# A two-layer decoder trunk: full-height query/key splits laid out by DMA, and attention outputs kept in device memory

## The chip, the cores and the metric

The kernel runs on one core of one Trainium2 chip. The metric is the device time of one execution in microseconds (us). In what follows PE is the matrix engine (TensorE), DVE the vector engine, ACT the scalar engine, POOL the GpSimd engine, and SP the engine whose queue issues the DMAs. Each engine works through its own queue of instructions in order; an instruction whose inputs are not ready holds up all that stand behind it on that engine.

## The reference

The reference is a trunk of two layers on 512 positions of width 1024. Each layer is a token mixer, a squared-ReLU MLP and a gated input embedding. Cut to the part that the change touches:

```python
for i in range(2):
    hn = rmsnorm(h, norm_mix_g[i])
    if i == 0: h = h + even_mixer(hn, ...)   # 8 stick-breaking heads, 4 differential heads (2 maps each)
    else:      h = h + odd_mixer(hn, ...)    # 16 dilated heads, T5 bias added to the logits
    ...                                      # MLP, gated embedding
# in a mixer
q, k, v = split(hn @ w_in)                   # heads of 64 columns
sc = q @ k.T * scale (+ bias[rel])           # causal
o = softmax(sc) @ v                          # or stick-breaking weights, or a difference of two softmaxes
return o @ w_out
```

All of it is in fp32.

## The kernel before

A product in fp32 is made as three products of parts (`mm3`, L135): every operand is split into `hi`, its value rounded to the PE's fp32r type, and `lo`, what is left over; then hi·hi, hi·lo and lo·hi are added in PSUM. Activations lie transposed, features on the 128 partitions and the 512 positions along the free axis.

A mixer works on four groups of four heads (two pairs for the differential kind). For a group, `project` (L398) runs the V, Q and K projections, each from a 1 MB block of weights that is loaded by one DMA (`wload`, L112, two buffers `raw`) and split by ACT into `wh` (L122) and by POOL into `wl` (L126), with three buffers of each. The first group of a layer takes Q and K before V. Q and K each have two halves of 128 rows (two heads of 64 rows). `attend` (L538) makes the steps of the attention of a group: scores, softmax or scan, a transpose, the product with V. The projection of one group is interleaved with the attention of the group before (`interleave`, L157); a scheduler settles each engine's queue from that. So PE always has projection matmuls to set between the attention's short ones, and the scores of a group can start when the K half of that group has been laid out.

The layout is made by `evacuate` (L457). `f` is the projected half, scaled, in fp32 (DVE, L460, tile `tmp`, one buffer). The score of a head is two matmuls over 128 partitions: the stationary `qq` holds the head's q hi in one half of the partitions and q lo in the other, the moving operand is once `kh` (k hi in both halves) and once `klz` (k lo in the half of q hi, zeros in the other, L493 and L494). A Q half takes 2 ACT copies and 2 DVE subtractions on 64 partitions (L466, L467); a K half takes 4 ACT copies and 2 DVE subtractions (L474 to L476).

All DMAs are issued on SP's queue, in the order in which the scheduler set them: weight blocks (L114), bias tiles (L500, three buffers), projections of the embedding put to device memory (L356, tile `pjd`) and fetched later. `prepare` (L308), after the first group's projection in layer 0, makes the rows from which the bias tiles are read: it loads a table, one-hot rows and offsets (L311 to L316) and lambdas (L319), runs four small matmuls (L323), writes the rows to device memory (`urow`, L326). The softmax of a score (DVE, L508) needs its bias tile.

Attention outputs stay in eight tiles of SBUF (`oT`, L396). Six of them are split and go through the output projection (`out_first`, L630, and `spread`, L624) under the last group's attention; the last two follow at the end of the mixer.

Of the kernel before, what the change touches and what calls it, by code (L numbers as in the profile page):

```python
# [12 lines left out]
F32 = mybir.dt.float32  # L13
F32R = mybir.dt.float32r
I32 = mybir.dt.int32
AF = mybir.ActivationFunctionType
ALU = mybir.AluOpType
AX = mybir.AxisListType

P = 128  # L20
D = 1024
S = 512
KT = D // P
# [39 lines left out]
def trunk(  # L63
# [5 lines left out]
    nc = tc.nc  # L69
    uid = [0]  # L70

    def nm(s):
        uid[0] += 1
        return f"{s}_{uid[0]}"

    cpool = ctx.enter_context(tc.tile_pool(name="cpool", bufs=1))
    dpool = ctx.enter_context(tc.tile_pool(name="dpool", bufs=1, space=bass.MemoryType.DRAM))
    wpool = ctx.enter_context(tc.tile_pool(name="wpool", bufs=2))
    apool = ctx.enter_context(tc.tile_pool(name="apool", bufs=8))
    spool = ctx.enter_context(tc.tile_pool(name="spool", bufs=8))  # L80
# [2 lines left out]
    def const(shape, name, dtype=F32):  # L83
        return cpool.tile(shape, dtype, tag=name, name=name)

    T_BUFS = {"e": 5, "tmp": 1, "tmp2": 3}

    mix = []

    def t2k(tag, pool=None, dtype=F32):  # L90
        return (pool or (mix[0] if tag in ("tmp", "tmp2") else spool)).tile([P, S], dtype, tag=tag, name=nm(tag), bufs=T_BUFS.get(tag, 2))

    def col(name="c"):
        return spool.tile([P, 1], F32, tag="col", name=nm(name), bufs=24)
# [3 lines left out]
    def ps(tag):  # L98
        return psum.tile([P, S], F32, tag=tag, name=nm(tag), bufs=PS_BUFS[tag])
# [12 lines left out]
    def wload(src):  # L112
        raw = wpool.tile([P, src.shape[-1]], F32, tag="raw", name=nm("raw"), bufs=2)
        nc.sync.dma_start(raw, src)  # L114
        return raw
# [19 lines left out]
    def mm3(acc, lh, ll, rh, rl, start, stop):  # L135
        nc.tensor.matmul(acc, lh, rh, start=start, stop=False)  # L136
        nc.tensor.matmul(acc, lh, rl, start=False, stop=False)  # L137
        nc.tensor.matmul(acc, ll, rh, start=False, stop=stop)  # L138
# [30 lines left out]
    def split_tile(src, scale=None, bufs=8):  # L169
        hi = apool.tile([P, S], F32R, tag="hi", name=nm("hi"), bufs=bufs)  # L170
        lo = apool.tile([P, S], F32R, tag="lo", name=nm("lo"), bufs=bufs)
        if scale is None:
            nc.scalar.activation(hi, src, AF.Copy)
            nc.vector.tensor_tensor(lo, src, hi.bitcast(F32), op=ALU.subtract)
        else:
            last_split[:] = [nc.scalar.activation(hi, src, AF.Copy, scale=scale).ins]
            nc.vector.scalar_tensor_tensor(lo, src, scale, hi.bitcast(F32), op0=ALU.mult, op1=ALU.subtract)  # L177
        return hi, lo
# [159 lines left out]
    def ple_units(layer):  # L338
        raw = wpool.tile([P, 2 * KT * P], F32, tag="raw", name=nm("raw"), bufs=2)
        nc.sync.dma_start(raw[:, 0:2 * S].rearrange("p (k c) -> p k c", k=2), pT[layer].rearrange("k p c -> p k c"))  # L340
        ph, pl = wsplit(raw, 0, 2, S)
        raw = wload(w_proj[layer])
        for c in range(2):
            wh, wl = wsplit(raw, c, 2, 512)
            for i in range(4):
                acc = ps("mm")
                sl = slice(i * P, (i + 1) * P)
                for k in range(2):
                    if layer < DEPTH - 1:
                        mm3(acc, wh[:, k, sl], wl[:, k, sl], ph[:, k], pl[:, k], k == 0, k == 1)  # L350
                    else:
                        mm3(acc, ph[:, k, sl], pl[:, k, sl], wh[:, k], wl[:, k], k == 0, k == 1)
                    yield 2.0
                t = t2k("tmp2")
                nc.scalar.activation(t, acc, AF.Copy)
                nc.sync.dma_start(pjd[layer, 4 * c + i], t)  # L356

    KLB = 2
    kl_i = [0]


    def mixer(layer, norm, nxt):
        st = ExitStack()
        mpool = st.enter_context(tc.tile_pool(name=f"mpool{layer}", bufs=2))
        mix[:] = [mpool]

        klz = [[mpool.tile([P, S], F32R, tag=f"klz{s}{x}", name=nm("klz"), bufs=1) for x in range(KLB)]
               for s in range(2)]
        for x in range(KLB):
            nc.gpsimd.memset(klz[0][x][64:128].bitcast(F32), 0.0)  # L370
            nc.gpsimd.memset(klz[1][x][0:64].bitcast(F32), 0.0)
        NSLOT = 13
        pth = [mpool.tile([P, NSLOT, P], F32R, tag=f"pth{i}", name=nm("pth"), bufs=1) for i in range(2)]
        ptl = [mpool.tile([P, NSLOT, P], F32R, tag=f"ptl{i}", name=nm("ptl"), bufs=1) for i in range(2)]
# [18 lines left out]
            return w_in[layer, nblk[0] - 1]  # L393

        first = []
        oT = [mpool.tile([P, S], F32, tag=f"o{k}", name=nm("o"), bufs=1) for k in range(KT)]  # L396

        def project(g, cur):  # L398
            kind = "dil" if layer else ("sb" if g < 2 else "diff")
# [33 lines left out]
            heads = []  # L433
# [23 lines left out]
            def evacuate(isq, i, acc, qk, qscale):  # L457
                rstd = stat["rstd"]
                f = t2k("tmp")
                nc.vector.scalar_tensor_tensor(f, acc, qscale if isq else -0.5, rstd, op0=ALU.mult, op1=ALU.mult)  # L460
                lower, upper = slice(0, 64), slice(64, 128)
                if isq:
                    qq = []
                    for a, b in ((lower, upper), (upper, lower)):
                        q = mpool.tile([P, S], F32R, tag="qq", name=nm("qq"), bufs=6)
                        nc.scalar.activation(q[a], f[a], AF.Copy)  # L466
                        nc.vector.tensor_tensor(q[b], f[a], q[a].bitcast(F32), op=ALU.subtract)  # L467
                        qq.append(q)
                    qk.append(qq)
                else:  # L470
                    for s, (a, b) in enumerate(((lower, upper), (upper, lower))):
                        kl = klz[s][kl_i[0] % KLB]
                        kh = mpool.tile([P, S], F32R, tag="kh", name=nm("kh"), bufs=5)
                        nc.scalar.activation(kh[a], f[a], AF.Copy)  # L474
                        nc.scalar.activation(kh[b], f[a], AF.Copy)
                        nc.vector.tensor_tensor(kl[a], f[a], kh[a].bitcast(F32), op=ALU.subtract)  # L476
                        heads.append((qk[i][s], kh, kl))
                    kl_i[0] += 1
            cur.extend((g, kind, v, heads))
            if start:  # L480
                wide_i[0] = 0
# [56 lines left out]
        def attend(g, kind, v, heads):  # L538
# [37 lines left out]
            def combine(x):  # L576
                hi, lo = pth[pts[x]], ptl[pts[x]]
                if kind == "diff":
                    vh = lambda j: v[:, j, P * x:P * x + P]
                    vl = lambda j: v[:, j, 256 + P * x:256 + P * x + P]  # L580
                    op = pv([(vh, hi), (vh, lo), (vl, hi)])
                    o = oT[2 * g + x]
                    nc.scalar.activation(o, op, AF.Copy)
                    return
                vs = lambda j: v[:, j, P * x:P * x + P]
                op = pv([(vs, hi), (vs, lo)])
                a = slice(64 * (x % 2), 64 * (x % 2) + 64)
                b = slice(64 - 64 * (x % 2), 128 - 64 * (x % 2))
                o = oT[2 * g + x // 2]
                nc.scalar.activation(o[a], op[b], AF.Copy)  # L590
                nc.vector.tensor_tensor(o[a], op[a], o[a], op=ALU.add)

            def subnorm(x):
                o = oT[2 * g + x]
                hi, rs, lo = t2k("tmp2", dtype=F32R), t2k("tmp2"), t2k("tmp2", dtype=F32R)
                nc.scalar.activation(rs, o, AF.Square)
                nc.scalar.activation(hi, rs, AF.Copy)
                nc.vector.tensor_tensor(lo, rs, hi.bitcast(F32), op=ALU.subtract)
                mp = ps("pv")
                nc.tensor.matmul(mp, ones_r, hi, start=True, stop=False)  # L600
                nc.tensor.matmul(mp, ones_r, lo, start=False, stop=True)
                rsqrt(rs, t2k("tmp2"), mp, SUBLN_EPS, eps_s, scale=float(D // P))
                nc.vector.scalar_tensor_tensor(o, o, gsub, rs, op0=ALU.mult, op1=ALU.mult)

            def step(n):
                m = n - LAG
# [10 lines left out]

            return [(lambda n=n: step(n)) for n in range(QT * nh + LAG + PVLAG + (kind == "diff"))]

        groups = GROUPS[layer]  # L620
        tiles = [2 * g + d for g in groups for d in range(2)]
        ohl = []

        def spread(units, every):  # L624
            for x, cost in enumerate(units):
                if x % every == 0 and len(ohl) < 6:
                    ohl.append(split_tile(oT[tiles[len(ohl)]]))
                yield cost

        def out_first():  # L630
            ohl.extend(split_tile(oT[k]) for k in tiles[len(ohl):6])
            for c in range(4):
                for i, ws in enumerate(block(w_outa[layer, c], 6, P)):
                    acc = ps("mm")
                    yield from lin_units([acc], [ws], ohl, 0, 6, False)
                    nc.vector.tensor_tensor(h[2 * c + i], h[2 * c + i], acc, op=ALU.add)
# [364 lines left out]
```

## Time and profile before

| | |
|---|---|
| median of 3 runs (lowest, highest) | 1314.71 us (1312.79, 1315.17) |
| profiled execution, its own time | 1313.5 us |
| its span in the trace | 1311.6 us |
| PE busy | 1280.7 us (98% of the span) |
| DVE busy | 982.5 us (75%) |
| ACT busy | 686.4 us (52%) |
| POOL busy | 189.0 us (14%) |
| mean granted PE clock | 0.999 |
| DMAs on SP's queue | 198 rows, 132 MB |

The span is the time between the first and the last instruction in the trace. A busy time adds up the stretches in which an engine works at an instruction; what an engine is short of the span it waited or had nothing to do.

### The profile page before, as it was taken

The numbers are of one execution on the slowest core, as the hardware profiler recorded it, in microseconds if no ns is written. First come the engines' busy times: TensorE is split into PE (matmuls) and PEld (weight loads), VectorE is DVE, ScalarE is ACT, GpSimd is POOL, SyncE is SP. The second block draws the span as 40 slices with busy tenths as digits, with TensorE's granted clock in tenths as the row PEclk, the third lists the DMA queues.
The fourth block names the chain that finished last, engine by engine and source line by source line (L and its number), as shares of the span: only waits on it lengthen the run. The fifth ranks groups of instructions, "written<-read, shape, count | busy, mean of one in ns | idle before, by whom it ended". The sixth has DMA issues, their size and how long they took to land.

```text
span 1311.6 us, 18552 instructions
## 1 busy us (share of the span) xinstructions
PE 1280.7 (98%) x7224; PEld 1112.5 (85%) x7224; DVE 982.5 (75%) x1669; ACT 686.4 (52%) x1117; POOL 189.0 (14%) x160
## 2 busy tenths in 40 slices
PE   8999999999999999999999999999999999999997
PEld 6878787788998989988889899878899898898886
DVE  6688888867858859945667878886795795994566
ACT  6566768654534435334456667765454443433344
POOL 2333343420000000000014333332000000000001
PEclk9999999999999999999999999999999999999999
DMA  5321323223232232322432232211323223232241
GB/s 208 123 91 55 114 95 107 89 82 111 97 116 78 97 129 71 122 97 96 161 121 103 64 114 76 72 65 64 129 78 116 96 97 113 81 129 96 97 145 65
DMA packets 28041, 133.21 MB, mean 102 GB/s; under 512 B 3312, under 2 KB 4048, under 8 KB 15280
## 3 DMA queue, kind: packets, MB, share of 16 engines
q1 hardware_dynamic: 27952, 132.01, 29.0%
q8 instruction: 57, 0.93, 0.3%
q14 instruction: 32, 0.26, 0.1%
HBM read 125.63 MB, written 6.37 MB: 101 GB/s over the span
## 4 chain that ended last, share of the span: by engine, by line
PE 78%; DVE 12%; ACT 7%; issue 2%; DMA 1%; SPq 0%; ACTq 0%; DVEq 0%
PE mm L137 12%; PE mm L138 12%; PE mm L136 12%; PE tp L138 5%; PE tp L136 5%; PE tp L137 5%; PE sc L136 4%; PE sc L137 4%; PE sc L138 4%; PE pv L137 2%; PE pv L136 2%; PE pv L138 2%; PE pv L534 2%; DVE e L572 2%; PE tp L519 1%
## 5 line engine op out<-in xcount | busy, mean ns | idle before, releaser
L122 ACT ACTIVATE wh<-raw 128x1024 fp32r<-128x1024 f32 (+1 forms) x168 | 173.5, 1037 | 230.1 <-PE mm L137 72.6
L136 PE MATMUL mm<-hi,wh 128*128 128x512 f32 x564 | 222.3, 394 | 0.9 <-ACT wh L302 0.9
L126 POOL TENSOR_TENSOR wl<-raw,wh 128x512 fp32r<-128x512 f32 (+1 forms) x132 | 176.3, 1358 | 318.4 <-ACT wh L122 301.7
L137 PE MATMUL mm<-lo,wh 128*128 128x512 f32 x564 | 220.6, 391 | 0.3 <-DVE lo L177 0.3
L138 PE MATMUL mm<-hi,wl 128*128 128x512 f32 x564 | 220.5, 391 | 0.3 <-DVE wl L128 0.3
L128 DVE TENSOR_TENSOR wl<-raw,wh 128x1024 fp32r<-128x1024 f32 x102 | 124.4, 1222 | 40.3 <-ACT wh L122 33.9
L138 PEld LDWEIGHTS mm<-hi,wl 128*128 128x128 f32 x564 | 105.9, 188 | 23.5 <-DVE wl L128 0.7
L137 PEld LDWEIGHTS mm<-lo,wh 128*128 128x128 f32 x564 | 106.0, 188 | 20.9 <-DVE lo L177 1.5
L136 PEld LDWEIGHTS mm<-hi,wh 128*128 128x128 f32 x564 | 105.9, 188 | 20.5 <-ACT wh L302 1.1
L725 ACT ACTIVATE wh<-raw 128x1024 fp32r<-128x1024 f32 x48 | 50.7, 1057 | 70.7 <-PE sc L137 35.5
L138 PE MATMUL mm<-uh,wl 128*128 128x256 f32 (+1 forms) x288 | 86.6, 301 | 0.0
L137 PE MATMUL mm<-ul,wh 128*128 128x256 f32 (+1 forms) x288 | 86.6, 301 | 0.0
L136 PE MATMUL mm<-uh,wh 128*128 128x256 f32 (+1 forms) x288 | 86.6, 301 | 0.0
L511 ACT ACTIVATE e<-e,mn 128x128 f32<-128x128 f32 (+3 forms) x96 | 53.8, 560 | 52.2 <-DVE mn L508 51.9
L704 DVE TENSOR_TENSOR ul<-u,uh 128x1792 fp32r<-128x1792 f32 (+1 forms) x32 | 58.4, 1824 | 23.4 <-ACT uh L703 23.4
L703 ACT ACTIVATE uh<-u 128x1792 fp32r<-128x1792 f32 (+1 forms) x32 | 49.4, 1543 | 48.4 <-DVE u L699 48.2
L692 ACT ACTIVATE u<-u 128x512 f32<-128x512 f32 x64 | 39.4, 624 | 53.4 <-DVE u L691 53.4
L726 DVE TENSOR_TENSOR wl<-raw,wh 128x1024 fp32r<-128x1024 f32 x48 | 58.6, 1221 | 9.8 <-ACT wh L725 9.7
L138 PE MATMUL sc<-hi,wl 128*128 128x512 f32 x168 | 65.6, 390 | 0.0
L137 PE MATMUL sc<-lo,wh 128*128 128x512 f32 x168 | 65.4, 389 | 0.0
L136 PE MATMUL sc<-hi,wh 128*128 128x512 f32 x168 | 65.4, 389 | 0.0
L137 PE MATMUL mm<-wl,hi 128*128 128x256 f32 (+1 forms) x216 | 64.1, 297 | 0.4 <-DVE wl L128 0.4
(255 smaller groups left out, 3463.9 us busy)
## 6 DMA issues: line engine op xcount, KB each, us to landing
raw<-in_w_up_dram SPq DMA_DIRECT2D x32, 1024.0 KB, 4.8
raw<-in_w_down_dram SPq DMA_DIRECT2D x32, 1024.0 KB, 4.9
raw<-in_w_in_dram SPq DMA_DIRECT2D x23, 1024.0 KB, 4.9
raw<-in_w_gate_dram SPq DMA_DIRECT2D x8, 1024.0 KB, 5.0
bias<-urow SPq DMA_DIRECT2D x24, 256.0 KB, 3.3
raw<-in_w_outa_dram SPq DMA_DIRECT2D x8, 768.0 KB, 4.2
pjd<-tmp SPq DMA_DIRECT2D x16, 256.0 KB, 2.2
pj<-pjd SPq DMA_DIRECT2D x16, 256.0 KB, 4.0
```

The lines of the kernel that those rows point to most:

```text
L122: nc.scalar.activation(hi, src, AF.Copy)
L126: nc.gpsimd.tensor_tensor(lo[:, kx], src[:, kx], hi[:, kx].bitcast(F32), op=ALU.subtract)
L128: nc.vector.tensor_tensor(lo, src, hi.bitcast(F32), op=ALU.subtract)
L136: nc.tensor.matmul(acc, lh, rh, start=start, stop=False)
L137: nc.tensor.matmul(acc, lh, rl, start=False, stop=False)
L138: nc.tensor.matmul(acc, ll, rh, start=False, stop=stop)
L511: nc.scalar.activation(e[:, 0:n], e[:, 0:n], AF.Exp, scale=-1.0, bias=mn, accum_out=s)
L692: nc.scalar.activation(ui, ui, AF.Square, scale=0.5)
L703: nc.scalar.activation(uh[:, parts], u[:, parts], AF.Copy)
L704: nc.vector.tensor_tensor(ul[:, parts], u[:, parts], uh[:, parts].bitcast(F32), op=ALU.subtract)
L725: nc.scalar.activation(hi, src, AF.Copy)
L726: nc.vector.tensor_tensor(lo, src, hi.bitcast(F32), op=ALU.subtract)
```

## The change

`evacuate` splits a half by one full-height ACT copy and one full-height DVE subtraction into two tiles `hl` (four buffers), and lays the parts out by DMAs from SBUF to SBUF, 64 partitions by 512 columns (128 KB) each: 4 for a Q half, 8 for a K half, 24 for a group. `kl` now holds k lo in both halves, as `kh` holds k hi, so the tiles with zeros and their memsets are gone. The output tiles rotate through five buffers; each of the first six of a layer is put to device memory when it is done (`put_out`) and fetched back before it is split (`fetch`): 12 puts and 12 fetches of 256 KB in all. In `ple_units` every second tile comes from the `hl` buffers.

```diff
-    T_BUFS = {"e": 5, "tmp": 1, "tmp2": 3}
+    T_BUFS = {"e": 5, "tmp": 1, "tmp2": 3, "hl": 4, "o": 5}
...
-                t = t2k("tmp2")
+                t = t2k("hl" if i % 2 else "tmp2")
                 nc.scalar.activation(t, acc, AF.Copy)
                 nc.sync.dma_start(pjd[layer, 4 * c + i], t)
...
-        klz = [[mpool.tile([P, S], F32R, tag=f"klz{s}{x}", name=nm("klz"), bufs=1) for x in range(KLB)]
-               for s in range(2)]
-        for x in range(KLB):
-            nc.gpsimd.memset(klz[0][x][64:128].bitcast(F32), 0.0)
-            nc.gpsimd.memset(klz[1][x][0:64].bitcast(F32), 0.0)
...
                 f = t2k("tmp")
                 nc.vector.scalar_tensor_tensor(f, acc, qscale if isq else -0.5, rstd, op0=ALU.mult, op1=ALU.mult)
+                hi, lo = t2k("hl", dtype=F32R), t2k("hl", dtype=F32R)
+                nc.scalar.activation(hi, f, AF.Copy)
+                nc.vector.tensor_tensor(lo, f, hi.bitcast(F32), op=ALU.subtract)
                 lower, upper = slice(0, 64), slice(64, 128)
                 if isq:
                     qq = []
-                    for a, b in ((lower, upper), (upper, lower)):
+                    for s in (lower, upper):
                         q = mpool.tile([P, S], F32R, tag="qq", name=nm("qq"), bufs=6)
-                        nc.scalar.activation(q[a], f[a], AF.Copy)
-                        nc.vector.tensor_tensor(q[b], f[a], q[a].bitcast(F32), op=ALU.subtract)
+                        nc.sync.dma_start(q[lower].bitcast(F32), hi[s].bitcast(F32))
+                        nc.sync.dma_start(q[upper].bitcast(F32), lo[s].bitcast(F32))
                         qq.append(q)
                     qk.append(qq)
                 else:
-                    for s, (a, b) in enumerate(((lower, upper), (upper, lower))):
-                        kl = klz[s][kl_i[0] % KLB]
-                        kh = mpool.tile([P, S], F32R, tag="kh", name=nm("kh"), bufs=5)
-                        nc.scalar.activation(kh[a], f[a], AF.Copy)
-                        nc.scalar.activation(kh[b], f[a], AF.Copy)
-                        nc.vector.tensor_tensor(kl[a], f[a], kh[a].bitcast(F32), op=ALU.subtract)
-                        heads.append((qk[i][s], kh, kl))
-                    kl_i[0] += 1
+                    for x, s in enumerate((lower, upper)):
+                        both = []
+                        for tag, part in (("kh", hi), ("kl", lo)):
+                            k = mpool.tile([P, S], F32R, tag=tag, name=nm(tag), bufs=4)
+                            nc.sync.dma_start(k[lower].bitcast(F32), part[s].bitcast(F32))
+                            nc.sync.dma_start(k[upper].bitcast(F32), part[s].bitcast(F32))
+                            both.append(k)
+                        heads.append((qk[i][x], *both))
...
+        def put_out(k):
+            if k in tiles[:6]:
+                nc.sync.dma_start(od[k], oT[k])
+
+        def fetch():
+            if len(back) < 6:
+                back.append(t2k("o"))
+                nc.sync.dma_start(back[-1], od[tiles[len(back) - 1]])
+
+        def split_out():
+            if not back:
+                for _ in range(2):
+                    fetch()
+            ohl.append(split_tile(back[len(ohl)]))
+            fetch()
```

Rows on SP's queue go from 198 to 414. Three places of the scheduled queues follow; in them `raw` is a weight block, and numbers tell tiles of one name apart.

The first is SP's queue in layer 1, where the first group's attention gives way to the second's. Before, the load of the third group's K weights (`raw_7716`) stands between bias loads:

```order
L500 DMA bias_7406<-urow 128x512
L500 DMA bias_7544<-urow 128x512
L114 DMA raw_7716<-in_w_in_dram 128x2048
L500 DMA bias_7658<-urow 128x512
L114 DMA raw_7872<-in_w_in_dram 128x2048
```

With the change the eight copies of the second group's first K half stand directly behind the same load (`raw_7869` here):

```order
L496 DMA bias_7687<-urow 128x512
L114 DMA raw_7869<-in_w_in_dram 128x2048
L471 DMA kh_7340<-hl_7336 64x512
L472 DMA kh_7340<-hl_7336 64x512
L471 DMA kl_7343<-hl_7337 64x512
L472 DMA kl_7343<-hl_7337 64x512
L471 DMA kh_7346<-hl_7336 64x512
L472 DMA kh_7346<-hl_7336 64x512
L471 DMA kl_7349<-hl_7337 64x512
L472 DMA kl_7349<-hl_7337 64x512
L628 DMA od<-o_7328 128x512
```

So what ACT and DVE wrote in place is now issued by SP after that load. The same eight rows stand behind the next group's load of the same kind, 33 rows later; at the third such place of layer 1 a bias load and four fetches stand ahead of them, and no weight block.

The second is PE's queue at the same place: the product with V of the old group's last head, the third group's V projection (`mm`), and the first score (`sc`) of the new group. Before:

```order
L534 MATMUL pv_7255<-ptl_6471,v_6476 128x256
L136 MATMUL mm_7279<-wh_7281,hi_6087 128x256
L137 MATMUL mm_7279<-wl_7282,hi_6087 128x256
L138 MATMUL mm_7279<-wh_7281,lo_6088 128x256
L493 MATMUL sc_7291<-kh_7210,qq_7022 128x256
L494 MATMUL sc_7291<-klz_6361,qq_7022 128x256
L136 MATMUL mm_7279<-wh_7281,hi_6098 128x256
```

With the change:

```order
L530 MATMUL pv_7389<-ptl_6471,v_6476 128x256
L136 MATMUL mm_7422<-wh_7424,hi_6194 128x256
L137 MATMUL mm_7422<-wl_7425,hi_6194 128x256
L138 MATMUL mm_7422<-wh_7424,lo_6195 128x256
L136 MATMUL mm_7422<-wh_7424,hi_6205 128x256
L137 MATMUL mm_7422<-wl_7425,hi_6205 128x256
L138 MATMUL mm_7422<-wh_7424,lo_6206 128x256
L136 MATMUL mm_7422<-wh_7424,hi_6277 128x256
L137 MATMUL mm_7422<-wl_7425,hi_6277 128x256
L489 MATMUL sc_7434<-kh_7340,qq_7142 128x256
L138 MATMUL mm_7422<-wh_7424,lo_6278 128x256
```

The first score moved back by five matmuls; its second product, with `kl`, stands 13 rows behind it. The next group's transition has the same order.

The third is SP's queue at the start of layer 0, where `prepare` loads its rows (`e`) and lambdas (`tmp`). Before:

```order
L311 DMA e_514<-in_t_table_dram 32x16
L312 DMA e_511<-in_onehot_dram 32x512
L313 DMA e_514<-in_onehot_dram 32x128
L315 DMA e_512<-in_offs_dram 16x512
L315 DMA e_513<-in_offs_dram 16x512
L316 DMA e_514<-in_offs_dram 16x2x128
L114 DMA raw_968<-in_w_in_dram 128x2048
L319 DMA tmp_515<-in_lambdas_dram 128x256
```

With the change, all 24 copies of the first group stand between the second and the third of these loads:

```order
L311 DMA e_523<-in_t_table_dram 32x16
L312 DMA e_520<-in_onehot_dram 32x512
L462 DMA qq_324<-hl_320 64x512
L463 DMA qq_324<-hl_321 64x512
...
L471 DMA kl_393<-hl_387 64x512
L472 DMA kl_393<-hl_387 64x512
L313 DMA e_523<-in_onehot_dram 32x128
L315 DMA e_521<-in_offs_dram 16x512
L315 DMA e_522<-in_offs_dram 16x512
```

On PE, the 96 matmuls of the second group's V projection and 42 of its Q projection move ahead of the third score, which before stood behind some 60 matmuls of V alone; by the end of the second group's K projection the two orders have the same work behind them.

## Rows read from the trace of the kernel before

**Rows 1.** Page, part 1: busy time, share of the span, instructions.

```profile
PE 1280.7 (98%) x7224; PEld 1112.5 (85%) x7224; DVE 982.5 (75%) x1669; ACT 686.4 (52%) x1117; POOL 189.0 (14%) x160
```

**Rows 2.** Busy time by stretch: PE, PEld, DVE, ACT, POOL, clock, DMA share, GB/s.

```profile
50.00:100.00 50.00, 47.50 (x274) 40.14 (x273) 37.77 (x99) 32.65 (x71) 15.99 (x13) 1.00 0.31 101
200.00:250.00 50.00, 47.37 (x235) 37.79 (x233) 44.16 (x75) 35.97 (x76) 19.01 (x15) 1.00 0.31 106
750.00:800.00 50.00, 50.00 (x304) 44.19 (x303) 40.48 (x103) 35.11 (x78) 18.44 (x14) 1.00 0.25 85
```

**Rows 3.** Waits of PE, 0 to 310 us: total, times, longest.

```profile
PE tp L519 <- DVE ptl L524: 4.1, 6, 1.3
PE sc L493 <- DVE mn L508: 3.5, 3, 1.8
PE sc L493 <- ACT e L569: 2.4, 3, 1.2
...
PE sc L323 <- DVE v L431: 1.7, 1, 1.7
```

**Rows 4.** Waits of PE, 660 to 960 us.

```profile
PE sc L493 <- DVE mn L508: 1.3, 1, 1.3
PE sc L493 <- DVE v L431: 0.7, 1, 0.7
```

**Rows 5.** Groups by shape, `evacuate`: busy, mean ns | idle before, releaser.

```profile
L476 DVE TENSOR_TENSOR klz<-tmp,kh 64x512 fp32r<-64x512 f32 x32 | 33.6, 1049 | 7.9 <-ACT kh L474 7.5
L467 DVE TENSOR_TENSOR qq<-tmp,qq 64x512 fp32r<-64x512 f32 x32 | 31.9, 998 | 3.8 <-ACT qq L466 3.0
...
L475 ACT ACTIVATE kh<-tmp 64x512 fp32r<-64x512 f32 x32 | 20.1, 629 | 0.7
```

**Rows 6.** Timeline near 154 us, ACT then PE: start, duration, idle before.

```profile
151.71 0.63 ACT L475 ACTIVATE kh<-tmp 64x512 fp32r<-64x512 f32 x1
...
154.14 0.45 PE L493 MATMUL sc<-kh,qq 128*128 128x384 f32 x1 [1.18 <-ACT e L569]
```

**Rows 7.** Timeline 748 to 756 us: ACT, DVE, POOL, SP, PE.

```profile
748.01 1.05 ACT L122 ACTIVATE wh<-raw 128x1024 fp32r<-128x1024 f32 x1
...
748.78 0.67 DVE L460 SCALAR_TENSOR_TENSOR tmp<-mm,rstd 128x512 f32<-128x512 f32 x1
...
749.13 3.00 POOL L126 TENSOR_TENSOR wl<-raw,wh 128x512 fp32r<-128x512 f32 x2 [6.82 <-ACT wh L122]
...
752.16 0.33 SPq L114 DMA_DIRECT2D raw<-in_w_in_dram  x1
...
754.98 0.28 PE L493 MATMUL sc<-kh,qq 128*128 128x256 f32 x1
755.10 0.28 PE L494 MATMUL sc<-klz,qq 128*128 128x256 f32 x1
```

**Rows 8.** DMA issues, median us to landing: 752 to 752.5 us; then 166 to 170 us.

```profile
raw<-in_w_in_dram SPq DMA_DIRECT2D x1, 1024.0 KB, 5.0
...
raw<-in_w_in_dram SPq DMA_DIRECT2D x1, 1024.0 KB, 5.4
pjd<-tmp SPq DMA_DIRECT2D x1, 256.0 KB, 5.6
```

**Rows 9.** SP's timeline, 167.5 to 169 us; the page's DMA issues.

```profile
167.93 0.34 SPq L114 DMA_DIRECT2D raw<-in_w_in_dram  x1
168.38 0.37 SPq L356 DMA_DIRECT2D pjd<-tmp  x1
...
pjd<-tmp SPq DMA_DIRECT2D x16, 256.0 KB, 2.2
```

**Rows 10.** Timeline 40 to 54 us: PE, then DVE.

```profile
46.96 0.39 PE L323 MATMUL sc<-e 32*16 32x128 f32 x2 [1.68 <-DVE v L431]
...
40.87 0.69 DVE L460 SCALAR_TENSOR_TENSOR tmp<-sc,rstd 128x512 f32<-128x512 f32 x1
...
53.92 0.29 DVE L508 CUSTOM_DVE_ANT_0 e<-sc,bias 128x128 f32<-128x128 f32 x1 [2.50 <-PE mm L138]
```

More of the change, by code (lines that the diff above doesn't have):

```diff
@@ L84, in const @@
         return cpool.tile(shape, dtype, tag=name, name=name)
-    T_BUFS = {"e": 5, "tmp": 1, "tmp2": 3}
+    T_BUFS = {"e": 5, "tmp": 1, "tmp2": 3, "hl": 4, "o": 5}
     mix = []
     def t2k(tag, pool=None, dtype=F32):
-        return (pool or (mix[0] if tag in ("tmp", "tmp2") else spool)).tile([P, S], dtype, tag=tag, name=nm(tag), bufs=T_BUFS.get(tag, 2))
+        return (pool or (mix[0] if tag in ("tmp", "tmp2", "hl", "o") else spool)).tile([P, S], dtype, tag=tag, name=nm(tag), bufs=T_BUFS.get(tag, 2))
     def col(name="c"):
@@ L353, in ple_units @@
                     yield 2.0
-                t = t2k("tmp2")
+                t = t2k("hl" if i % 2 else "tmp2")
                 nc.scalar.activation(t, acc, AF.Copy)
                 nc.sync.dma_start(pjd[layer, 4 * c + i], t)
-    KLB = 2
-    kl_i = [0]
+    od = dpool.tile([KT, P, S], F32, tag="od", name="od")
     def mixer(layer, norm, nxt):
@@ L395, in mixer @@
         first = []
-        oT = [mpool.tile([P, S], F32, tag=f"o{k}", name=nm("o"), bufs=1) for k in range(KT)]
+        oT = {}
         def project(g, cur):
@@ L581, in combine @@
                     op = pv([(vh, hi), (vh, lo), (vl, hi)])
-                    o = oT[2 * g + x]
+                    o = oT[2 * g + x] = t2k("o")
                     nc.scalar.activation(o, op, AF.Copy)
@@ L588, in combine @@
                 b = slice(64 - 64 * (x % 2), 128 - 64 * (x % 2))
+                if x % 2 == 0:
+                    oT[2 * g + x // 2] = t2k("o")
                 o = oT[2 * g + x // 2]
@@ L591, in combine @@
                 nc.vector.tensor_tensor(o[a], op[a], o[a], op=ALU.add)
+                if x % 2:
+                    put_out(2 * g + x // 2)
             def subnorm(x):
@@ L603, in subnorm @@
                 nc.vector.scalar_tensor_tensor(o, o, gsub, rs, op0=ALU.mult, op1=ALU.mult)
+                put_out(2 * g + x)
             def step(n):
@@ L621, in mixer @@
         tiles = [2 * g + d for g in groups for d in range(2)]
-        ohl = []
+        ohl, back = [], []
+        def put_out(k):
[11 more added lines that the diff above has]
+            fetch()
         def spread(units, every):
@@ L626, in spread @@
                 if x % every == 0 and len(ohl) < 6:
-                    ohl.append(split_tile(oT[tiles[len(ohl)]]))
+                    split_out()
                 yield cost
         def out_first():
-            ohl.extend(split_tile(oT[k]) for k in tiles[len(ohl):6])
+            while len(ohl) < 6:
+                split_out()
             for c in range(4):
```

## The prediction

> **What bounds the kernel now.** I read the page's busy times first. PE is busy 1280.7 of 1311.6 us [rows 1], so at most 31 us of the span are idle on PE, and only time added to PE's queue or taken out of its waits counts. Then busy time by stretch, to see which parts of the mixers have slack: in layer 0 PE misses 2.5 us between 50 and 100 and 2.6 between 200 and 250, where DVE is busy 44.2 of 50 us; in layer 1, from 750 to 800, PE misses nothing at all, though DVE does 40.5 of 50 [rows 2]. So in layer 1 there is nothing to win, and any new wait is a plain loss; in layer 0 there is a little to win from a lighter DVE and ACT. Then the waits of PE, for what that little is made of: in layer 0 tp behind DVE's ptl 4.1 us, scores behind DVE's softmax 3.5, scores behind ACT's e 2.4, one wait of 1.7 of a small matmul behind a v [rows 3]; in layer 1 1.3 and 0.7 [rows 4]. Last the timelines of ACT, DVE, POOL, SP and PE where one group's attention gives way to the next, since the edit sits there.
>
> The sum is made against the profiled execution, 1313.5 us; the median of the runs shown, 1314.7, is 1.2 above it, and I add the difference found to the median.
>
> **What is taken away.** The half-height operations go: 64 on DVE with 33.6 and 31.9 us busy, and 96 on ACT of 0.63 us, of which one of three groups is shown [rows 5]. Full-height ones over the same 512 columns replace them, 32 on each engine. I take one to cost as much as a half-height one, since the columns are as many. DVE then loses 65.5/2 = 32.7 us over eight groups, 4.1 a group; ACT 64 x 0.63 = 40 us, 5.0 a group. None of this is PE time, so it is worth what it takes out of PE's waits:
> - The score at 154.14 waited 1.18 us for ACT's e, and ACT had come from the last of its four kh copies at 152.34 [rows 6]. With one copy in place of four it is about 1.9 us earlier there. Of the 2.4 us of such waits [rows 3] I take 1.8 off.
> - The small matmul of `prepare` that waited 1.7 us for a v [rows 3, 10] now stands 75 rows behind its fellow, with projection work between: 1.7 off.
> - The wait of layer 1's first score for a v, 0.7 [rows 4], lies behind the same subtractions on DVE: 0.7 off.
> - The waits for DVE's ptl and softmax, 4.1 + 3.5 + 1.3 = 8.9 us [rows 3, 4]. DVE sheds 4.1 of about 41 us a group, a tenth, but the waits are chains that pass through ACT too. I take 2.0 off; the bounds are 0 and 8.9.
>
> Together 6.2 us, with bounds 0 and 13.7. The eight memsets on POOL were on no path.
>
> **What is added, layer 1.** SP now issues the copies, in order. At the transition before 755 us two chains start from the last matmul of a K half: the projection's f (DVE, 748.78 to 749.45), and the release of a `wh` buffer, so ACT's L122 at 748.01, POOL's L126 until 752.13, and then SP's load of a K block at 752.16 [rows 7]. With the change the second half of the first chain, the eight copies, stands on SP directly behind that load. The split itself could be done near 751 (0.67 for f, then 0.63 and 0.69), so the copies wait for the load to be issued, and then for its bytes. The load lands 5.0 us after its issue, at 757.16 [rows 8]. What a 256 KB transfer does right behind a 1 MB load is shown at 168 us: the load issued at 167.93 landed after 5.4, at 173.33; pjd, issued at 168.38, took 5.6 and landed at 173.98, 0.65 behind it, where pjd's median is 2.2 [rows 8, 9]. So the small transfer waited in line for the large one. The two copies of kh are 256 KB too: they land at about 757.16 + 0.65 = 757.8. PE came to its first score at 754.98 [rows 7]; five more matmuls stand ahead of it now, at 0.12 us each by the starts of such matmuls [rows 7]: 755.6. The stall is 2.2 us. The kl copies land 0.65 later, at 758.5; their matmul stands 13 rows on, at 757.8 + 1.6 = 759.4, and doesn't wait. Bounds: if copies did not stand in line, they would land 2.2 after an issue at 753.1 (two issues at the pace of 0.45 of rows 9), 755.3, and nothing is lost; if each needed pjd's 5.6 from there, 758.7, and 3.1 is lost. The same order stands at the next group's transition, 48 us later; at the third no weight block is ahead. Two stalls: 4.4 us, with bounds 0 and 6.2. PE had no idle time there to take it up [rows 2].
>
> What would a half-height copy cost? [...] No row here shows a copy on 64 partitions between tiles of SBUF. [...]
>
> **What is added, layer 0.** At the start, 24 copies stand between two loads of `prepare`. The last eight follow the second K half, whose f starts at 40.87 [rows 10]; split, it is ready near 43, and eight issues at 0.45 end at 46.6, four more loads at 48.4, and they land 2.2 to 5.6 later [rows 8, 9]: 50.6 to 54. Before, it was 7.0 us from the small matmul at 46.96 to the first softmax at 53.92 [rows 10]; so the first softmax comes at 57.6 to 61, 4 to 7 us late. PE has the second group's V and most of a Q half to do meanwhile, so it doesn't stall then. But the attention of the first group is pressed into less time: DVE's 37.8 us [rows 2], less 4.1, in 39 to 42 us, 80 to 87%, about the load at which PE misses 2.6 us in 50 from 200 to 250, against 2.5 already missed here [rows 2]. I take 1.5; the bounds are 0 (hidden) and 7 (nothing is made up).
>
> Other transitions of layer 0 have their copies landed 1 us or more before the first score by the same reckoning. The 12 puts and 12 fetches of 256 KB lie on SP under projections that are tens of us long; the fetches are asked for before the output projection's weights. A copy of the embedding's projection on ACT can wait for an `hl` buffer that the copies still read. 0.5 us for all that, with bounds 0 and 2.
>
> **Sum.** 4.4 + 1.5 + 0.5 - 6.2 = +0.2 us: 1313.7 against 1313.5, or 1314.9 against the median. Within 0.2% (2.6 us) a measurement of this kernel can't tell it from no change. I forecast 1315.
>
> **Rivals.**
> 1. *The copies are hidden and the lighter engines pay.* If copies don't stand in line behind a weight block (the nearest row against it is pjd at 168 us [rows 8]), the two stalls are nothing; if also half of the 8.9 us goes instead of 2.0, relief is 8.7. With 1.5 for the start and 0.5: -6.7, 1308. For it: DVE at 44.2 of 50 in layer 0 is the second engine there. Against it: layer 1 has no idle PE time to win. 33%.
> 2. *Copies on 64 partitions are slow.* If each takes twice as long, kh lands 1.3 behind the block, the stalls rise by 1.4, and the 24 copies of the start, 12 pairs at 0.65 = 7.8 us of transfer, take 15.6: the first softmax is 8 us later still and the start costs its upper bound of 7. +7.1, 1322. It decides from about 1 us a pair on. 15%. [...]
> 3. *Weight blocks come late (slower).* SP's queue is in order, so a block that stands behind copies or a put waits for DVE's and ACT's results of that group. A block takes 5.0 to land, 1.05 and 3.0 to split [rows 7, 8], so 9 us ahead of its first matmul its issue has no slack left; each us past that is lost. If each of six blocks that follow copies in the queue came 1 us past its slack: +6, 1321. It decides when a put waits for an output that is later than the split. Against it: a block's issue waits first for POOL's split of the one two before [rows 7], which leaves the copies time. 15%.
>
> **How the numbers follow.** The forecast has 37% and reaches over 0.2% to either side (1312 to 1317). Faster by over 0.2% is rival 1, 33%; slower are rivals 2 and 3, 30%. The range takes in the three at their worked-out times: from 1307.5 (rival 1, with the rounding of its sum) to 1322.
>
> **What would show it.** In the profile after: waits of PE for kh at L489 of about 2 us at two places in layer 1, spans of kh copies that end just behind the block ahead of them; the wait of L323 gone; ACT's wait at 154 gone; the first L508 near 60 us; DVE's busy time lower by about 33 us and ACT's by 40. Wrong would be: full-height operations that cost twice a half-height one (no relief), copies that take far longer than 0.65 a pair, or waits of PE for `wh` in the mixers.

## The result and the profile after

Over 16 runs each the changed kernel took 1317.46 us (1314.66 to 1321.43) and the kernel before 1315.16 us (1312.79 to 1317.06): a ratio of 1.0022, with a 95% interval of 1.0013 to 1.0030. So it is slower by about 2.3 to 2.9 us, which is at the edge of the 0.2% that I called no change (the interval lies on both sides of it), and inside the range given. The profiled execution took 1319.5 us, with a span of 1317.8: 6.2 above that of before. Executions of one kernel differ together with their mean granted clock (of the change the fastest took 1314.66 us at 0.995, the slowest 1321.43 at 0.991), and the profile of the change (0.991) is one of its slower ones, that of before (0.999) one of its faster ones, so a difference of two profiles is not that of the medians.

The page's busy times, to be held against [rows 1]:

```profile
PE 1286.2 (98%) x7224; PEld 1119.0 (85%) x7224; DVE 949.2 (72%) x1637; ACT 646.7 (49%) x1053; POOL 181.5 (14%) x152
```

DVE lost 33.3 us and ACT 39.7, as worked out. But PE, with the same 7224 matmuls, is busy 5.5 us longer. Its idle time is 1317.8 - 1286.2 = 31.6 us against 30.9: as much as before, though made of other things. The busy times by stretch (columns as in [rows 2]) show where:

```profile
50.00:100.00 50.00, 49.13 (x286) 41.33 (x285) 34.59 (x105) 26.53 (x65) 16.60 (x12) 1.00 0.69 195
200.00:250.00 50.00, 45.18 (x213) 36.59 (x212) 36.69 (x68) 30.81 (x68) 15.34 (x14) 0.93 0.58 182
750.00:800.00 50.00, 46.55 (x276) 41.85 (x275) 33.84 (x93) 27.02 (x63) 13.81 (x10) 0.93 0.54 156
800.00:850.00 50.00, 46.90 (x281) 41.79 (x280) 33.12 (x92) 26.32 (x62) 16.25 (x12) 0.97 0.50 143
```

Between 50 and 100 us PE now misses 0.87 us where it missed 2.5. At three later places it misses 3 us and more, and there the clock column, 1.00 in the same stretches before, falls to 0.93 and 0.97. Layer 1's mixer can be compared as a whole: the stretch from the 3600th to the 5200th matmul takes it in, and begins and ends in long products in which PE is full in both kernels. Before, then with the change (columns as in [rows 2]; PEld's count is that of the matmuls):

```profile
666.24:958.34 292.10, 289.43 (x1601) 248.66 (x1600) 230.11 (x501) 186.64 (x369) 81.74 (x68) 1.00 0.27 91
664.36:964.77 300.41, 292.80 (x1602) 252.86 (x1600) 215.43 (x485) 167.93 (x337) 78.13 (x64) 0.98 0.47 140
```

So the change comes to this stretch 1.9 us earlier than the kernel before and loses 8.3 us in it. The waits of PE from 0 to 310 us (columns as in [rows 3]):

```profile
PE sc L489 <- DMA kh<-hl: 3.1, 1, 3.1
PE tp L515 <- DVE ptl L520: 2.8, 4, 1.3
PE mm L136 <- ACT hl L355: 2.6, 2, 2.3
```

And from 660 to 960 us:

```profile
PE sc L489 <- DMA kh<-hl: 6.5, 2, 3.5
PE tp L515 <- DVE e L557: 0.6, 1, 0.6
```

The waits of [rows 3, 4] for DVE's softmax, ACT's e, and a v are gone, ptl's fell from 4.1 to 2.8. In their place stand three waits for kh, 9.6 us in all, and 2.6 for L355. The timelines of the first layer-1 place answer to [rows 7] (POOL, DVE, SP, then PE):

```profile
745.53 3.00 POOL L126 TENSOR_TENSOR wl<-raw,wh 128x512 fp32r<-128x512 f32 x2 [5.98 <-ACT wh L122]
...
746.61 0.77 DVE L456 TENSOR_TENSOR hl<-tmp,hl 128x512 fp32r<-128x512 f32 x1
...
748.56 0.34 SPq L114 DMA_DIRECT2D raw<-in_w_in_dram  x1
748.99 0.47 SPq L471 DMA_DIRECT2D kh<-hl  x1
749.51 0.59 SPq L472 DMA_DIRECT2D kh<-hl  x1
...
756.30 0.55 PE L489 MATMUL sc<-kh,qq 128*128 128x256 f32 x1 [3.45 <-DMA kh<-hl]
756.65 0.41 PE L138 MATMUL mm<-wh,lo 128*128 128x256 f32 x1
756.86 0.41 PE L136 MATMUL mm<-wh,hi 128*128 128x256 f32 x1
```

Both parts of the K half were ready at 747.38 (746.61 + 0.77), and the copies went out at 748.99, behind the weight block that POOL's split released at 748.53. The landings (columns as in [rows 8]), of the block and of either kh copy:

```profile
raw<-in_w_in_dram SPq DMA_DIRECT2D x1, 1024.0 KB, 6.7
...
kh<-hl SPq DMA_DIRECT2D x1, 128.0 KB, 6.7
```

The block landed at 755.26, the second kh copy at 749.51 + 6.7 = 756.2, and PE went on at 756.30, as in the chain that was forecast. Behind the stall one more thing is to be seen: matmuls that started 0.12 us apart before [rows 7] now start 0.21 apart. The busy times in slices of one microsecond (the column 1.00, 0.64, 0.50 is the granted clock):

```profile
754.00:755.00 1.00, 0.00 (x0) 0.00 (x0) 0.17 (x1) 0.00 (x0) 0.57 (x1) 1.00 1.02 254
755.00:756.00 1.00, 0.00 (x0) 0.00 (x0) 0.00 (x0) 0.00 (x0) 0.00 (x0) 0.64 1.06 287
756.00:757.00 1.00, 0.70 (x3) 0.73 (x4) 0.00 (x0) 0.00 (x0) 0.00 (x0) 0.50 1.02 260
...
761.00:762.00 1.00, 1.00 (x7) 1.00 (x7) 0.38 (x4) 0.60 (x2) 0.00 (x0) 0.50 0.81 191
762.00:763.00 1.00, 1.00 (x9) 1.00 (x9) 0.40 (x1) 0.00 (x0) 0.00 (x0) 0.94 0.87 201
```

While PE stood idle the granted clock fell to 0.50, and it stayed there from about 755.3 to 762.1 (0.64 is a slice with 0.72 us at the lower level, 0.94 one with 0.12), so for 5.8 us of full work after PE went on. The same view shows 2.9 us of work at 0.50 behind the second stall of layer 1 (3.10 us, near 808) and 6.5 us behind the one in layer 0 (3.08 us, near 208). I estimate from the 0.50 that half of such work was lost, 2.9 + 1.4 + 3.3 = 7.6 us in all, if PE is what everything waits for there; by the starts behind the first stall, 0.21 us apart for 0.12, it was 43%.

### The profile page after: what moved, and what is told of

Same layout as the page of the kernel before. It is cut to its first block, busy times and chain, and to the rows that moved or that the text cites. A ratio compares the mean times of both kernels' runs of the same rounds, so it can differ in the third digit from the quotient of the medians.

```text
span 1317.8 us, 18911 instructions
## 1 busy us (share of the span) xinstructions
PE 1286.2 (98%) x7224; PEld 1119.0 (85%) x7224; DVE 949.2 (72%) x1637; ACT 646.7 (49%) x1053; POOL 181.5 (14%) x152
## 4 chain that ended last, share of the span: by engine, by line
PE 82%; DVE 8%; ACT 4%; DMA 2%; issue 2%; SPq 1%; POOL 0%; ACTq 0%; DVEq 0%
PE mm L136 13%; PE mm L138 13%; PE mm L137 13%; PE tp L136 5%; PE tp L138 5%; PE tp L137 5%; PE sc L138 5%; PE sc L136 5%; PE sc L137 5%; PE pv L137 2%; PE pv L138 2%; PE pv L136 2%; PE pv L530 2%; PE tp L515 2%; DMA kh<-hl 1%
## 5 line engine op out<-in xcount | busy, mean ns | idle before, releaser
L126 POOL TENSOR_TENSOR wl<-raw,wh 128x512 fp32r<-128x512 f32 (+1 forms) x132 | 172.9, 1331 | 332.8 <-ACT wh L122 329.7
L136 PE MATMUL mm<-wh,hi 128*128 128x256 f32 (+1 forms) x216 | 65.6, 304 | 2.3 <-ACT hl L355 2.3
```

The lines of the kernel that those rows point to most:

```text
L126: nc.gpsimd.tensor_tensor(lo[:, kx], src[:, kx], hi[:, kx].bitcast(F32), op=ALU.subtract)
```

## The experiments

My theory after the result (A): lighter ACT and DVE gave about 10 us, and three stalls of PE for kh behind a weight block, with the low clock behind each, took a little more than that back. Rivals: (B) the copies, puts and fetches cost the time as added DMA load, so that moving them helps little; (C) idle time alone counts; (D) the copies' place behind the block on SP's queue is not what delays them.

**Layer 1's copies first.** The block's load is ordered on SP behind the first four copies of the K half that is needed next. Nothing else is changed in the code.

```diff
+            for c in behind:
+                order(load.ins, c)
...
-                    blk = ... block(src, KT, P)
+                    blk = ... block(src, KT, P, () if isq or layer not in (1,) else kfirst)
...
+                            if i == 0 and x == 0:
+                                kfirst.extend((c1.ins, c2.ins))
```

> In layer 1 the load of a K block is ordered behind the first four copies of the K half that PE needs next; layer 0 is left as in the change. Theory A: the change lost its gain to three stalls of PE for kh (3.45, 3.10 in layer 1, 3.08 in layer 0), each with a weight block ahead of the copies on SP, and to the stretches at a granted clock of 0.50 behind them (6.4 and 3.4 us in layer 1, half of which is lost). Then both stalls of layer 1 and their slow stretches go: 6.5 + 4.9 = 11.4 us, 1317.5 to 1306. Rival C, the idle time alone counts and the clock is another matter: -6.5, 1311. Rival B, the copies are slow as such or the added DMA load costs the time: the waits for kh stay and the time is 1316 to 1318.

Measured: 1306.58 us, ratio to before 0.9937 (0.9923 to 0.9952). Against the change that is 1.0022 - 0.9937 = 0.85%, 11.2 us, where A said 11.4 and C 6.5. Its busy times by stretch:

```profile
750.00:800.00 50.00, 50.00 (x313) 44.69 (x312) 36.98 (x101) 29.43 (x68) 18.09 (x13) 1.00 0.59 161
800.00:850.00 50.00, 49.37 (x291) 42.91 (x290) 38.71 (x106) 31.11 (x73) 14.28 (x12) 1.00 0.61 176
```

At the first place of layer 1 SP now issues the copies when the parts are ready, and the load long after (SP and PE):

```profile
743.23 0.46 SPq L477 DMA_DIRECT2D kh<-hl  x1
743.74 0.59 SPq L478 DMA_DIRECT2D kh<-hl  x1
...
748.71 0.28 PE L497 MATMUL sc<-kh,qq 128*128 128x256 f32 x1
...
756.54 3.44 SPq L116 DMA_DIRECT2D raw<-in_w_in_dram  x2
```

The kh copies landed after 2.3 us, where they had taken 6.7. No wait for kh is left in layer 1, the clock stays at 1.00, and PE is full again from 750 to 800, with DVE at 37.0 where it had 40.5 [rows 2]. Not all of the 11.2 us need be layer 1's, for in layer 0 the wait of 3.08 for kh near 208 is gone in this profile too (0.2 for kl is left), though its order was not touched. Layer 1's mixer by itself, in the same stretch of matmuls as above, settles it:

```profile
660.99:950.58 289.59, 288.55 (x1601) 248.98 (x1600) 214.49 (x485) 168.15 (x337) 78.73 (x64) 1.00 0.49 146
```

It takes 300.4 - 289.6 = 10.8 us less than with the change. So the two stalls with their slow stretches are shown to be worth about 11 us, more than their 6.5 us of idle time; 6.5 and half of the 8.7 us of work at the lower clock make 10.9 (A's expectation counted the time at the lower clock otherwise and came to 11.4). Rivals B and C fall.

**All copies first.** K blocks of both layers, and in layer 0 the first block of the output projection, are ordered behind copies.

```diff
-                for i, ws in enumerate(block(w_outa[layer, c], 6, P)):
+                for i, ws in enumerate(block(w_outa[layer, c], 6, P, kfirst if c == 0 and layer == 0 else ())):
```

> As the run before, and in layer 0 too, where the first block of the output projection is held behind the copies. Theory A: the third stall (3.08) and its slow stretch (6 us at 0.50, 3.0 lost) go as well: another 6.1 us, 1300. Rival C: 1308. Rival B: 1316 to 1318. If the held block comes late, a wait of PE for wh in the output projection stands in place of the stall and the gain over the run before is under 3 us.

Measured: 1307.84 us, ratio 0.9949 (0.9935 to 0.9962). No gain over the run before. As that run had no wait for kh at the third place in its profile, this one doesn't price A's 6 us; it shows only that nothing more is to be had there by ordering. From 200 to 250 PE is busy 44.85 us here, 47.04 in the run before; waits for DVE, ACT and POOL stand there. Layer 0 gives up one wait for another.

**No copies at all.**

```diff
+                if isq:
+                    qk.append(hi)
+                else:
+                    heads.extend(((qk[i], hi, lo), (qk[i], hi, lo)))
```

> The copies are left out: the scores read the two full-height parts as they are, so that the two heads of a half use the same operands and the scores are sums over both heads; the instructions on PE, ACT and DVE are as many as in the change. It prices full-height splits without any layout. Theory A: no stall for kh, no slow stretch, and the 2.6 us of waits behind L355 gone: the relief of ACT and DVE alone, which A puts at 11 to 12 us (idle of PE fell by 9.0 beside stalls of 9.6 and waits of 2.6... of the old kind), so 1300 to 1304, as good as the run with the copies first. Rival B: much lower than that run, by 10 us or more, since the copies cost what they move. If the relief is no more than the 6.2 of the prediction: 1309.

The rest of the edit gives the parts tiles of their own (eight of each kind), and the embedding's projection its tile from `tmp2`; puts and fetches stay.

Measured: 1304.96 us, ratio 0.9926 (0.9914 to 0.9939). This is what the lighter ACT and DVE are worth without any layout, with these tiles: 0.74%, 9.7 us. The waits of PE that are left in layer 0, and layer 1's mixer:

```profile
PE tp L502 <- DVE ptl L507: 2.8, 4, 1.3
PE sc L476 <- DVE mn L491: 2.5, 3, 1.6
PE mm L136 <- ACT tmp L355: 1.9, 2, 1.5
PE sc L476 <- ACT e L552: 1.6, 1, 1.6
...
662.44:950.91 288.47, 287.95 (x1601) 249.14 (x1600) 214.34 (x485) 167.78 (x338) 78.87 (x64) 1.00 0.30 103
```

The run with layer 1's copies first lies 1.6 us above it by the medians, with overlapping intervals, and 1.1 us in layer 1's mixer: 24.6 MB of copies cost next to nothing here, where no weight block stands ahead of those that PE needs next.

**The copies of the first K half on ACT's queue.**

```diff
-                            nc.sync.dma_start(k[lower].bitcast(F32), part[s].bitcast(F32))
-                            nc.sync.dma_start(k[upper].bitcast(F32), part[s].bitcast(F32))
+                            queue = nc.sync if i or start else nc.scalar
+                            queue.dma_start(k[lower].bitcast(F32), part[s].bitcast(F32))
+                            queue.dma_start(k[upper].bitcast(F32), part[s].bitcast(F32))
```

> The copies of the first K half of each group but the first are issued by ACT's queue instead of SP's, all else as in the change. Theory A in the form that a queue is a line of its own (the copies wait because they are behind the block on SP): the stalls for kh go, 1317.5 to about 1302, a little more than the run with the copies first since ACT pays eight issues a group. Rival D, all queues share the DMA engines and a block's bytes go first anyway: PE still waits for kh 2 us or more at the same places, 1312 or above.

Measured: 1335.02 us, ratio 1.0152 (1.0138 to 1.0166), the slowest of all. Its timelines at the first layer-1 place (ACT's queue, SP's, PE, ACT):

```profile
754.80 0.47 ACTq L472 DMA_DIRECT2D kh<-hl  x1
...
756.01 0.56 ACTq L472 DMA_DIRECT2D kl<-hl  x1
756.61 0.61 ACTq L473 DMA_DIRECT2D kl<-hl  x1
...
756.75 0.34 SPq L114 DMA_DIRECT2D raw<-in_w_in_dram  x1
...
764.48 0.35 PE L491 MATMUL sc<-kl,qq 128*128 128x256 f32 x1 [4.86 <-DMA kl<-hl]
...
764.61 0.60 ACT L520 ACTIVATE pth<-tp 128x512 fp32r<-128x512 f32 x1 [9.84 <-DMA kl<-hl]
```

And its DMA issues: the kh copy of 754.80, then from 756.7 to 757 us the block and the kl copy of 756.61:

```profile
kh<-hl ACTq DMA_DIRECT2D x1, 128.0 KB, 2.2
...
raw<-in_w_in_dram SPq DMA_DIRECT2D x1, 1024.0 KB, 7.3
kl<-hl ACTq DMA_DIRECT2D x1, 128.0 KB, 7.7
```

The copies no longer wait for the load to be issued: kh went out at 754.80, 1.95 us ahead of the block, landed after 2.2, and PE didn't wait for it here or at the next place of this kind. At the third the first kh copy and a block were issued together, at 864.61; there kh took 6.8 and PE waited 3.2 for it. But the kl copy of 756.61 was issued only 0.14 us ahead of the block, on another queue, and took 7.7 us: it landed at 764.3 with the block, which landed at 756.75 + 7.3 = 764.05. The kl copy at 756.01, 0.74 us ahead of the block, took 2.4. So the other queue was no way past the block; to be issued 0.74 us ahead of it was. Neither A in its form of a line on SP nor D is right as it stands: the line on SP's queue set when the copies were issued, and a copy issued on ACT's queue beside the block still took 7.7 us. That agrees with D's assumption that the queues share the DMA engines, which no run shows by itself. Besides, ACT issued its eight copies in line with its own work and stood 9.84 us, nearly half of it before the eighth, which went out at 764.10, as the block landed; why it waited for that is not shown. So PE waited 13.3 us for kl and kh in layer 1, and 6.2 at one place of layer 0 for a result of ACT.

**Puts and fetches alone.** The kernel before, with rotating output tiles, `put_out` and `fetch`, and nothing else of the change.

> The kernel before with one part of the change alone: output tiles rotate through five buffers, the first six of a layer go to device memory and are fetched back. Splits and layout as before. The prediction put this and the hl buffers together at 0.5 us (0 to 2). If it is hidden: 1314 to 1316, ratio within 0.2% of 1. Rival B (the added DMA load costs the time): 1317 or more.

Measured: 1315.13 us, ratio 1.0000 (0.9990 to 1.0011). They are hidden, to within 0.1%, in the kernel before.

**The embedding's tile, and K blocks in both layers.** Two runs in which `ple_units` takes its tile from `tmp2` alone; the first also orders the K blocks of layer 0 behind copies.

```diff
-                t = t2k("hl" if i % 2 else "tmp2")
+                t = t2k("tmp2")
```

> K blocks of both layers behind the first four copies of the K half before; the output projection's first block is not held, and the embedding's projection takes its tile from tmp2 alone, as before the change. If the held block of the output projection cost what kept the run with all copies first from being faster than that of layer 1 alone, and the waits of 2.6 us behind L355's tile go: 1303 to 1304. If waits only move within layer 0: 1306 to 1308.

Measured: 1310.01 us, ratio 0.9960 (0.9947 to 0.9972).

> The run with layer 1's copies first (1306.6), and the embedding's projection takes its tile from tmp2 alone. If the wait of 2.3 us for L355 near 157 us was for an hl tile that pending copies still read, it goes: 1304, and the granted clock stays at 0.999 there. If PE then reaches the third place (near 206) earlier and waits there for kh behind the output projection's block, the time is 1306 to 1308.

Measured: 1310.22 us, ratio 0.9961 (0.9948 to 0.9973), against 0.9937 without the edit, with intervals that just overlap. In the profiles both take 289.59 us for layer 1's mixer, and the one with the edit comes to it 3.4 us later. The wait for L355 (L359 in these runs) went and another of the same length came. PE's timeline in the run with layer 1's copies first:

```profile
159.34 0.39 PE L140 MATMUL mm<-wh,hi 128*128 128x256 f32 x1 [2.34 <-ACT hl L359]
```

And in the second of these two runs:

```profile
157.81 0.63 PE L523 MATMUL tp<-ident,e 128*128 128x128 f32 x4 [2.36 <-DVE e L577]
```

There PE waits for the step behind the stick-breaking scan on DVE, and that scan had itself waited 1.21 us for ACT. Both runs came out above either branch of what was expected (1304, or 1306 to 1308); what the edit costs in layer 0 stays open.

**Wide copies.** One copy of 128 partitions in place of two of 64; both heads of a half read the same keys.

```diff
-                            nc.sync.dma_start(k[lower].bitcast(F32), part[s].bitcast(F32))
-                            nc.sync.dma_start(k[upper].bitcast(F32), part[s].bitcast(F32))
+                            nc.sync.dma_start(k.bitcast(F32), part.bitcast(F32))
```

> The change with each pair of 64-partition copies of a K part replaced by one copy of the whole part, 128 partitions and the same 256 KB; so both heads of a half read the same keys, and the scores are not those of the reference. Same order on SP, behind the same weight blocks, half as many DMAs. If 64-partition copies move at a lower rate than 128-partition ones (kh landed 0.95 us behind the block in the change, where pjd, 128 partitions, took 0.65), kh lands 0.3 to 0.5 earlier behind the block and the two stalls of layer 1 are about 3.0 and 2.7 instead of 3.45 and 3.10: 1316 to 1317. If the stall is the block's own landing, slowed from 5.0 to 6.7 by the copies' bytes, it stays within 0.2: 1317 to 1318.

Measured: 1324.47 us, ratio 1.0068 (1.0055 to 1.0082), slower than the change. Its timeline at the first layer-1 place, SP, then PE:

```profile
752.35 0.34 SPq L114 DMA_DIRECT2D raw<-in_w_in_dram  x1
752.78 0.48 SPq L471 DMA_DIRECT2D kh<-hl  x1
...
759.88 0.35 PE L488 MATMUL sc<-kh,qq 128*128 128x256 f32 x1 [3.87 <-DMA kh<-hl]
```

The landings of these two:

```profile
raw<-in_w_in_dram SPq DMA_DIRECT2D x1, 1024.0 KB, 6.8
kh<-hl SPq DMA_DIRECT2D x1, 256.0 KB, 7.0
```

kh landed 759.78 - 759.15 = 0.63 behind the block, the 0.65 that pjd had shown [rows 8], where the pair of half-height copies took 0.95. So the half-height pair did cost 0.3 us more, about half as much again; whether by its 64 partitions or by being two DMAs is not separated. But the block itself landed after 6.8 us, as with the narrow copies, and the stall is no shorter. The expectation of a shorter one failed, and the time lies above what either branch gave; most of the extra time of this kernel lies at 50 to 100 us, where PE is busy 43.9 of 50, and I did not follow that up.

**More hl buffers, fewer output buffers.** Layer 1's copies first, with 5 and 4, then 6 and 3, in place of 4 and 5.

```diff
-    T_BUFS = {"e": 5, "tmp": 1, "tmp2": 3, "hl": 4, "o": 5}
+    T_BUFS = {"e": 5, "tmp": 1, "tmp2": 3, "hl": 5, "o": 4}
```

> The run with layer 1's copies first (1306.6) with five hl buffers in place of four and four output buffers in place of five. If the wait of 2.3 us of PE near 157 us in that run is for want of an hl tile whose copies are pending, one more buffer shortens it: 1303 to 1305, and the slow stretch behind it goes. If four output buffers make outputs wait for their put: a new wait of PE or ACT for o, 1308 or more. If waits only move within layer 0, as when the tile came from tmp2 (1310): 1306 to 1310.

> The same with six hl and three output buffers. If hl buffers are what layer 0 lacks: as the run with five or better, 1302 to 1305. If three output buffers are too few for puts and fetches: slower than the run with five, by a wait for o at the output projection's splits.

Measured: 1307.09 us, ratio 0.9940 (0.9928 to 0.9953), and 1306.53 us, ratio 0.9936 (0.9923 to 0.9950): as with 4 and 5. The longest wait for L355's tile fell from 2.3 to 0.6 and 0.5, and the time stayed. So that wait was not what held the time.

The version to keep is layer 1's copies first: 0.63% faster than before and 0.85% faster than the change.

## Why the prediction was right or wrong

- **Relief.** The busy time that it takes off DVE and ACT was right (32.7 and 40 worked out, 33.3 and 39.7 measured). Its worth was put at 6.2 us. Without copies it is 9.7 by the medians, and 1311.6 - 1303.9 = 7.7 by the spans of the two profiles. The mis-sized term is the one for waits behind DVE's softmax and ptl, from which I took 2.0 of 8.9: without copies 2.8 and 2.5 are left of them, so 3.6 went. ACT's e gave 0.8 where 1.8 was taken; the two waits for a v went as worked out. That is 6.8 by the named waits. The 2.0 between medians and profiles go with the granted clock, which was 0.995 to 0.998 in the executions of before beside that run (0.999 in the profile of before) and 0.998 to 0.999 without copies; no run isolates them. That "in layer 1 there is nothing to win" was wrong: its mixer takes 3.6 us less without copies (292.1 and 288.5). It was read from 750 to 800 us alone, and the sum had 0.7 there, and a share of the 2.0.
- **Two stalls in layer 1.** Place, cause and order were right, and at the third transition, with no block ahead, PE didn't wait, as said; the size was not right. 2.2 us each were forecast, 3.45 and 3.10 measured. PE came to the first score 4.3 us after the block's issue (752.85), where 3.4 was worked out, which made the stall shorter by 0.9; kh landed 7.6 after that issue, where 5.65 was worked out. Of that 1.7 is the block itself, which landed after 6.7 us, with copies beside it, in place of the 5.0 of [rows 8], and 0.3 is the half-height pair.
- **The clock.** The step "at 0.12 us each" took the granted clock for constant. It fell to 0.50 in each of the three stalls, of 3.45, 3.10 and 3.08 us, and the 128x256 matmuls behind the first started 0.21 us apart where they had started 0.12 apart. The first experiment prices both stalls at 11.2 us (10.8 in layer 1's mixer) where 4.4 stood in the sum. Of the difference some 2 us are the longer stalls and some 4 the clock, the term that was missing.
- **Other transitions of layer 0, "1 us or more before the first score".** Wrong for the last: there the output projection's block, issued at 200.10, stands ahead of the copies issued from 202.18 on, and PE waited 3.08. The block took 8.7 us to land there and kh 6.8; in the run with layer 1's copies first, with the same order in layer 0, they took 5.5 and 3.8, and no wait for kh was left. That, and that ordering it away won nothing, leaves open what this stall is worth.
- **The late start.** The first softmax came at 66.81, later than the 57.6 to 61 worked out, and cost nothing: PE missed 0.87 us from 50 to 100 where it had missed 2.5 [rows 2]. The projection work that moved ahead covered it, so the 1.5 us of the sum were not paid.
- **Puts, fetches and L355.** 0.5 us was forecast; puts and fetches alone cost nothing, L355's wait is 2.6, but its removal brings others.
- **The rivals.** The first (1308) had the relief about right and the stalls wrong; with layer 1's copies first the time is 1306.6. The second fails: a pair of copies landed 0.95 behind the block, not 1.3, and the start, for which it charged 7 us, cost nothing. No run shows the factor of two in its 1.3 and 15.6; the pair took 1.5 times the 0.63 of one 128-partition copy of the same bytes. The third fails: in the change's profile no wait of PE for a weight block in the mixers is listed beyond 0.4 us.
- **The sum.** +0.2 was forecast, +2.9 by the ratio. Two errors partly cancel: 3.5 us too little relief, and some 7 us too little for the two stalls. The mechanism of the stalls was foreseen; that the sum came so near is in part luck.

## What to carry to other kernels

A small DMA that the bottleneck waits for should be issued well ahead of a large load (here a copy issued on another queue 0.74 us ahead landed after 2.4 us, one 0.14 us ahead after 7.7, and one on the same queue 0.43 us behind after 6.7); DMAs are best looked at in the issue order of all queues together, and holding one load of a group behind four copies repaired here what 24 MB of added traffic seemed to cost. The two stalls of PE, of 3.45 and 3.10 us, cost 1.6 to 1.7 times their length, since the clock of 0.50 behind them had to be paid as well. Removing a wait in layer 0, where DVE is 83% busy and ACT 64% (100 to 250 us with layer 1's copies first), brought another of the same length in these runs; only the run that leaves the work out tells what is to be had.

## What the hardware showed that I had not expected

- In this change's profile the granted clock fell from 1.00 to 0.50 during idle times of PE of 3.1 to 3.45 us, and stayed there for 2.9 to 6.5 us after PE went on, while it was fully busy. Waits of 2.3 us were followed by it in one profile (0.50 from about 160.5 to 164 with layer 1's copies first) and not in another (the change, 2.28 us up to 159.49, with 1.00 from 154 to 163).
- A 1 MB load alone landed after 5.0 us, beside eight copies of 128 KB after 6.4 to 6.7, beside copies of another queue after 7.3.
- A copy that another engine's queue issued 0.14 us ahead of such a load landed with it, after 7.7 us; one issued 0.74 us ahead took 2.4. A pair of 64-partition copies landed 0.95 us behind a load, one 128-partition copy of the same bytes 0.63.
